# A one-core two-layer hybrid kernel: gathered-row dots pinned to program order and paced anew, gather credits raised, modulation rows placed elsewhere

## The chip, the cores and the metric

The kernel runs on one core of one Trainium2 chip, so all engines named below (TensorE = PE, VectorE = DVE, ScalarE = ACT, GpSimd = POOL, SyncE = SP) are those of a single core. The metric is the device time of one execution in microseconds (us); the median of repeated runs is compared.

## The reference

Two layers, each a mixer followed by a feed-forward part, on 512 tokens of width 1024. Layer 0 mixes with a gated linear recurrence (LRU), layer 1 with an attention with a forget gate (FoX). Both feed-forward parts are PEER: each token picks 16 of 16,384 experts for each of 8 heads, and an expert is one row of `u` and one row of `v`. Ahead of each part the token is normed and modulated by a shift, a scale and a gate that come from one vector `c`.

```python
for layer in range(DEPTH):
    shift, scale, gate = ada_modulation(c, mw, mb)     # silu(c) @ mw + mb
    h = rms_norm(x, g) * (1.0 + scale) + shift
    x = x + gate * mixer(h, ...)                       # rglru or fox
    shift, scale, gate = ada_modulation(c, mw2, mb2)
    h = rms_norm(x, g2) * (1.0 + scale) + shift
    x = x + gate * peer_ffn(h, ...)

# peer_ffn, for 128 tokens:
q = (xc @ q_w).reshape(TOKEN_CHUNK, PEER_HEADS, 2, PEER_HALF)
...                                                    # two top-16 searches, then top-16 of sums
expert = e1 * PEER_KEYS + e2                           # 128 experts for each token
g = jax.nn.softmax(top_s, axis=-1)
u = jnp.take(expert_u, expert, axis=0)
act = gelu(jnp.einsum('thkd,td->thk', u, xc))
w = g * act
return jnp.einsum('thk,thkd->td', w, jnp.take(expert_v, expert, axis=0))
```

## The kernel before

The 512 tokens are four tiles of 128. PEER treats them in two ways. For the first three tiles (`nd` = 3) it computes **all** experts densely: 128 blocks of 128 experts each, where a block's up-projection (`pacc`, L509 to L511, three matmul terms of split fp32) gives activations, these are multiplied by a dense table of gates, and the result is multiplied by the block of `v` into `vacc` (L1263). For the last tile (t = 3) it **gathers** instead (`gathered`): POOL issues an indirect DMA for each of the 128 picked rows of `u` (L1141), DVE takes the dot of that row with the token (L1154), and later the same for 128 rows of `v`, which DVE accumulates with a weight (L1171). The gathered rows live in a ring of 8 buffers (`RING`).

A third way stands in between: the last 32 rows of tile 2 (`XT`) are not in the dense table but go through `looked_up`: 32 dots (L1031) of rows that POOL gathers (L1016), first into 13 borrowed buffers, then into a small pool `xr` of three.

PEER runs in stages. First come the queries. Then comes the **gates stage**: 68 of the blocks (`NFIRST`) have their up-projection computed early and stored to HBM (`ascr`), and beside them run the routes (top-k searches on DVE), the three `dense_gates` generators and `looked_up`. `dense_gates(t)` builds the table for one token tile from batches of 16 tokens: DVE makes one-hot tiles `p2` and `p1` by comparing with an iota (L1115, L1118), multiplies `p1` with the gates in two precisions into two `pg` tiles (L1126; `gp`, L1084 and L1085, is the gates' split), and PE multiplies them (L1100). Then comes the **expert loop** over 128 blocks in which a block's activations are loaded back (`at<-ascr`, on ACT's queue) or computed, multiplied with the gate tile `gtile` (L1249), split (L1253 on ACT, L1256 on DVE) and multiplied by `v` (L1263). Every weight of the dense products is split into `whi` (ACT, L185) and `wlo` (DVE, L187).

Three kinds of side work are written as generators and mixed into these loops by credit. A `Background` holds a list of generators; `pump(credit)` adds credit and runs units until it is spent, and each unit costs what it yields. `GP` is the credit per stored block in the gates stage; `PUMPS` holds for each layer the credit per block of the expert loop (first number: block not stored; second: block stored). `between_steps(main, side, (a, b))` runs `looked_up` as the side of the other generators: each side unit costs a before `xr` exists, and b after it. What is left at a loop's end is run by `bg.finish()` right there, ahead of the work that follows.

The third kind is the modulation: one dot of a 1024-long weight row `mw` with `c` for each of 128 outputs (L220, then one or two small column operations L224 to L227), and one load of 0.5 MB for each row on POOL's queue (`mod_gen`). `AT` cuts the 24 rows of `l1_mix` into those done in the LRU's output projection, those in the first PEER's loop (`between`), and the rest; `M1` does the same for the 6 first rows of `l1_ffn`, which are done after the first PEER's gathered rows (`last_rows`).

The kernel is scheduled by a framework that may move an instruction ahead of others on its engine; `keep_in_program_order` (often called `pin`) forbids that. At run time each engine's queue is in order: an instruction that waits for a DMA holds all behind it.

## Time and profile before

| | |
|---|---|
| median of 3 runs | 3128.37 us (3125.5 to 3131.63) |
| profiled execution | 3128.77 us |
| its span in the trace | 3127.0 us (so 1.8 us lie outside it) |
| ScalarE busy | 1490.6 us (48%) |
| GpSimd busy | 1055.3 us (34%) |
| DMA moved | 855.28 MB, mean 274 GB/s |

In the trace the stages of layer 0 lie at about 0 to 205 us (norm and LRU), 205 to 270 (LRU's output projection), 270 to 440 (norm and PEER's queries), 440 to 775 (gates stage), 775 to 1500 (expert loop). FoX follows to 1824, with its output projection to 1870; the second PEER has its queries up to 2040, its gates stage from 2040 to 2365 and its expert loop from 2365 to 3105. The last stretch to 3127 is the end of that loop's adds and the stores.

How to read it: PE is busy most of the time in every stage, so what counts is where PE stands still and who releases it. A row of the timeline gives start, duration, engine, line, operation and tile, and in brackets the idle time ahead of the instruction on its engine with the work that ended it. A row of the windows gives a stretch, its length, then for each engine the busy us and the number of instructions, then the granted clock of PE, the busy share of the DMA engines, and GB/s.

### The profile page before, as it was taken

How to read it: one execution, taken by the hardware profiler on the slowest of the kernel's cores; microseconds unless marked ns; L12 is line 12 of the kernel's file. 1: busy time of each engine (PE TensorE's matmuls, PEld its weight loads, DVE VectorE, ACT ScalarE, POOL GpSimd, SP SyncE). 2: the span in 40 equal slices, each digit the busy share in tenths (PEclk: the TensorE clock that was granted, in tenths of full speed). 3: DMA queues.
4: the chain of work that ended last, by engine and by line, in shares of the span. 5: the costliest groups of instructions: out<-in, count | busy, mean ns of one | idle time of the engine just before them, and what ended most of it. 6: DMA issues, size and time to landing. Idle time of an engine off the chain costs nothing.

```text
span 3127.0 us, 45280 instructions
## 1 busy us (share of the span) xinstructions
PE 2981.9 (95%) x16232; PEld 2624.3 (84%) x16232; DVE 2623.0 (84%) x5368; ACT 1490.6 (48%) x2432; POOL 1055.3 (34%) x906
## 2 busy tenths in 40 slices
PE   8999999988999999999999999999889999999996
PEld 6777899978888888888777778899888888888885
DVE  7867989877889889989779968898877888888888
ACT  6654244676333333333458843255684333433331
POOL 1001433201655525655011003422104444445454
PEclk9998999999999999999999999999999999999998
DMA  7554248877999999999532123377879999999998
GB/s 291 173 184 172 101 152 293 294 248 258 413 376 397 380 352 393 373 364 348 190 119 82 62 108 117 125 267 263 271 247 372 362 350 366 366 358 370 355 335 291
DMA packets 307938, 855.28 MB, mean 274 GB/s; under 512 B 27296, under 2 KB 162496, under 8 KB 268928
## 3 DMA queue, kind: packets, MB, share of 16 engines
q1 hardware_dynamic: 67280, 388.77, 32.9%
q0 software_dynamic: 98624, 354.99, 30.3%
q10 hardware_dynamic: 141808, 108.63, 10.5%
q8 instruction: 127, 2.08, 0.3%
q14 instruction: 99, 0.81, 0.1%
HBM read 767.93 MB, written 83.51 MB: 272 GB/s over the span
## 4 chain that ended last, share of the span: by engine, by line
PE 42%; DVE 25%; issue 15%; DMA 10%; ACT 4%; POOL 3%; ACTq 0%; DVEq 0%; SPq 0%; POOLq 0%
PE vacc L1263 16%; DMA at<-ascr 6%; PE pacc L511 6%; PE pacc L509 6%; PE pacc L510 6%; DVE wlo L187 4%; DVE accg L1171 3%; DVE rows L1154 2%; POOL rows L1141 2%; DVE pg L1126 2%; DMA rowx<-in_l_u_dram,eix 1%; DVE p L1118 1%; POOL rowx L1016 1%; DVE p L1115 1%; DVE mw L220 1%
## 5 line engine op out<-in xcount | busy, mean ns | idle before, releaser
L511 PE MATMUL pacc<-hhi,wlo 128*128 128x352 f32 (+1 forms) x2600 | 891.7, 343 | 15.4 <-DVE wlo L187 14.7
L509 PE MATMUL pacc<-hhi,whi 128*128 128x352 f32 (+1 forms) x2600 | 895.6, 344 | 9.7 <-ACT at L1242 6.9
L185 ACT ACTIVATE whi<-wraw 128x1024 fp32r<-128x1024 f32 (+1 forms) x646 | 662.0, 1032 | 481.3 <-PE pacc L510 271.1
L510 PE MATMUL pacc<-hlo,whi 128*128 128x352 f32 (+1 forms) x2600 | 889.1, 342 | 0.0
L187 DVE TENSOR_TENSOR wlo<-wraw,whi 128x1024 fp32r<-128x1024 f32 (+2 forms) x580 | 698.7, 1211 | 143.0 <-ACT whi L185 140.7
L1263 PE MATMUL vacc<-wlo,wh 128*128 128x512 f32 x1536 | 599.2, 390 | 4.9 <-DVE wlo L187 4.9
L1263 PE MATMUL vacc<-whi,wh 128*128 128x512 f32 x1536 | 599.4, 390 | 1.6 <-ACT wh L1253 0.9
L1263 PE MATMUL vacc<-whi,wl 128*128 128x512 f32 x1536 | 598.7, 390 | 0.0
L511 PEld LDWEIGHTS pacc<-hhi,wlo 128*128 128x128 f32 x2600 | 493.4, 190 | 45.4 <-DVE wlo L187 22.4
L509 PEld LDWEIGHTS pacc<-hhi,whi 128*128 128x128 f32 x2600 | 494.3, 190 | 36.6 <-ACT at L1242 7.8
L510 PEld LDWEIGHTS pacc<-hlo,whi 128*128 128x128 f32 x2600 | 495.4, 191 | 25.9
L1253 ACT ACTIVATE wh<-at 128x384 fp32r<-128x384 f32 x256 | 134.2, 526 | 778.2 <-DVE at L1249 611.7
L1141 POOL DMA_INDIRECT rows<-in_l_v_dram,ei x256 | 375.4, 1466 | 324.8 <-DVE accg L1171 273.5
L1141 POOL DMA_INDIRECT rows<-in_l_u_dram,ei x256 | 367.9, 1437 | 301.8 <-DVE rows L1154 251.8
L1263 PEld LDWEIGHTS vacc<-wlo,wh 128*128 128x128 f32 x1536 | 289.4, 188 | 62.6 <-DVE wlo L187 6.8
L1263 PEld LDWEIGHTS vacc<-whi,wl 128*128 128x128 f32 x1536 | 288.9, 188 | 60.3
L1263 PEld LDWEIGHTS vacc<-whi,wh 128*128 128x128 f32 x1536 | 288.9, 188 | 58.5 <-ACT wh L1253 1.3
L1171 DVE SCALAR_TENSOR_TENSOR accg<-rows,act,accg 128x1024 f32<-128x1024 f32 x254 | 324.8, 1279 | 0.6
L1154 DVE SCALAR_TENSOR_TENSOR rows<-rows,hn 128x1024 f32<-128x1024 f32 x256 | 305.2, 1219 | 2.4 <-issue 1.2
L1249 DVE TENSOR_TENSOR at<-at,gtile 128x384 f32<-128x384 f32 x256 | 141.1, 553 | 168.5 <-DMA at<-ascr 155.3
L1102 ACT ACTIVATE st<-gps 128x512 f32<-128x512 f32 x192 | 185.4, 1111 | 40.0 <-PE gps L1100 28.2
L187 POOL TENSOR_TENSOR wlo<-wraw,whi 128x1024 fp32r<-128x1024 f32 (+1 forms) x62 | 125.3, 2032 | 181.4 <-ACT whi L185 181.4
(335 smaller groups left out, 3639.4 us busy)
## 6 DMA issues: line engine op xcount, KB each, us to landing
wraw<-in_l_uT_dram SPq DMA_DIRECT2D x128, 1024.0 KB
wraw<-in_l_vp_dram SPq DMA_DIRECT2D x128, 1024.0 KB
gscr<-st ACTq DMA_DIRECT2D x48, 1024.0 KB
gtile<-gscr SPq DMA_DIRECT2D x90, 512.0 KB
mw<-in_l_ffn_mw_dram POOLq DMA_DIRECT2D x48, 512.0 KB
ascr<-at ACTq DMA_DIRECT2D x136, 176.0 KB
at<-ascr ACTq DMA_DIRECT2D x136, 176.0 KB
mw<-in_l_mix_mw_dram POOLq DMA_DIRECT2D x32, 512.0 KB
```

Of the source, the lines that this page charges most:

```text
L185: self.pin(nc.scalar.activation(hi, raw, AF.Copy))
L187: self.pin((nc.gpsimd if self.on_pool else nc.vector).tensor_sub(lo, raw, hi))
L509: nc.tensor.matmul(ps, whi[:, k, :], hhi[:, k, :n], start=(k == 0), stop=False)
L510: nc.tensor.matmul(ps, whi[:, k, :], hlo[:, k, :n], start=False, stop=False)
L511: nc.tensor.matmul(ps, wlo[:, k, :], hhi[:, k, :n], start=False, stop=(k == KD - 1))
L1102: A.activation(st[:, :, q * 4:q * 4 + 4].rearrange("p e t -> p t e"), gps, AF.Copy, scale=1.0 / GSCALE)
L1141: i = nc.gpsimd.indirect_dma_start(out=rows, out_offset=None, in_=src, in_offset=bass.IndirectOffsetOnAxis(ap=ei[:, j:j + 1], axis=0))
L1154: V.scalar_tensor_tensor(r, r, 1.0, hn, op0=OP.mult, op1=OP.mult, accum_out=act[:, j:j + 1]))
L1171: i = V.scalar_tensor_tensor(acc, r, w, acc, op0=OP.mult, op1=OP.add)
L1249: pin(V.tensor_tensor(at.rearrange("p (b t) -> p b t", t=16), at.rearrange("p (b t) -> p b t", t=16), gts[c // 8][:, :, c % 8, :], op=OP.m ...
L1253: pin(A.activation(wh, at, AF.Copy))
L1263: T.matmul(acc[t][d], x[:, ts], y[:, d, :], start=(i == 0 and x is wh and y is vh), stop=(i == PK - 1 and x is wl))
```

## The change

Counts of instructions on each engine stay the same. The change does four things. It raises the credits of the expert loops (`PUMPS`) and of the gates stage (`GP`), with slightly higher costs for the route's units. It changes the side credits of `looked_up` from (6.2, 4.2) to (6.8, 3.3), adds two empty units to it, and pins its dots and the operations of `dense_gates` to program order. It moves two modulation rows of `l1_mix` from the LRU's output projection into the first PEER's loop, gives those that stay four buffers and a delay by credit (`later`). And it moves the first six rows of `l1_ffn` from the end of the first PEER to the output projection of FoX.

```diff
--- before.py
+++ after.py
@@ -37,15 +37,15 @@
 XT = 32
 EARLY = (4, 0, 0, 2, 0, 2, 2, 2)
 NEARLY = sum(EARLY)
-PUMPS = ((4.45, 1.4), (3.9, 1.2))
+PUMPS = ((4.55, 1.5), (4.2, 1.35))
 AHEAD = 6
-GP = 5.2
+GP = 5.35
 GSCALE = 32768.0
 M1 = 6
 RING = 8
 MB = 2
 LP = 1.55
-AT = (4, 14)
+AT = (4, 12)
 
 
 class Ctx:
@@ -228,6 +228,10 @@
         if k + bufs < len(rows):
             got.append(load(rows[k + bufs]))
         yield unit
+
+
+def later(credit):
+    yield credit
 
 
 def row_of(g, psum, col, name):
@@ -959,14 +963,14 @@
             V.tensor_tensor(ge2, ge, row[:, :n], op=OP.mult)
             V.tensor_tensor(ge, ge, tab[0], op=OP.mult)
             fold(ge, n, ranks(e[0], q))
-            yield (5.5, 6.6)[q]
+            yield (6.0, 7.2)[q]
             j = rs.tile([128, HK], BF, name="j", tag="j")
             fold(ge2, n, j.rearrange("p (h k) -> p h k", h=PH))
             V.tensor_sub(j, posb, j)
             V.tensor_tensor(ge, j.unsqueeze(1).to_broadcast(shp), col[:, :n], op=OP.is_equal)
             V.tensor_tensor(ge, ge, tab[1], op=OP.mult)
             fold(ge, n, ranks(e[1], q))
-            yield (5.0, 7.6)[q]
+            yield (5.5, 8.4)[q]
 
         def route(t):
 
@@ -985,11 +989,12 @@
                 ei = (pk if t >= nd else rt).tile([128, 128], I32, name="ei", tag="ei" if t >= nd else "back")
                 V.scalar_tensor_tensor(ei, e[0], float(PK), e[1], op0=OP.mult, op1=OP.add)
                 e.append(ei)
-            yield 2.0
+            yield 2.2
 
         def looked_up(t, pu, pw, psum):
 
 
+            pin = tc.keep_in_program_order
             gt, ei = routes[t][2:]
             own = slice(128 - XT, 128)
 
@@ -1023,17 +1028,19 @@
             for s in range(SG - 1):
                 nc.scalar.dma_start(hn[s * XT:(s + 1) * XT], hn[own])
             yield 0.1
+            yield 0.1
             for j in range(XT):
                 for _ in range(2):
                     if len(rows) < (XT if "xr" in env else 13):
                         fetch(len(rows))
                 r = rows[j]
-                V.scalar_tensor_tensor(r, r, 1.0, hn, op0=OP.mult, op1=OP.mult, accum_out=act[:, j:j + 1])
-                yield 1.35 if "xr" in env else 2.7
+                pin(V.scalar_tensor_tensor(r, r, 1.0, hn, op0=OP.mult, op1=OP.mult, accum_out=act[:, j:j + 1]))
+                yield 1.35 if "xr" in env else 2.9
             A.activation(act, act, AF.Gelu)
             back = rt.tile([128, 128], F32, name="back", tag="back")
             for s in range(SG):
                 nc.scalar.dma_start(back[own, s * XT:(s + 1) * XT], act[s * XT:(s + 1) * XT])
+            yield 0.1
             V.tensor_mul(back[own], back[own], gt[own])
             most = rt.tile([128, 1], F32, name="mostc")
             V.memset(most, 1.0)
@@ -1081,8 +1088,9 @@
             for w in range(2):
                 A.activation(edup[w], tp[:, w, :].unsqueeze(2).to_broadcast(shp), AF.Copy)
             gp = [pu.tile([128, 128], F16, name=f"gp{i}", tag=f"gp{i}") for i in range(2)]
-            V.tensor_scalar(gp[0], tp[:, 2, :], GSCALE, None, op0=OP.mult)
-            V.scalar_tensor_tensor(gp[1], tp[:, 2, :], GSCALE, gp[0], op0=OP.mult, op1=OP.subtract)
+            pin = tc.keep_in_program_order
+            pin(V.tensor_scalar(gp[0], tp[:, 2, :], GSCALE, None, op0=OP.mult))
+            pin(V.scalar_tensor_tensor(gp[1], tp[:, 2, :], GSCALE, gp[0], op0=OP.mult, op1=OP.subtract))
             gdup = []
             for i in range(2):
                 d = pu.tile(shp, F16, name=f"gdup{i}", tag=f"gdup{i}")
@@ -1112,10 +1120,10 @@
                 def spread(x):
                     return x[:, bs, :].unsqueeze(1).to_broadcast(shp)
                 p2 = pw.tile(shp, F16, name="p2", tag="p2")
-                V.tensor_tensor(p2, iota_e.unsqueeze(1).to_broadcast(shp),
-                                edup[1][:, bs, :].unsqueeze(2).to_broadcast(shp), op=OP.is_equal)
+                pin(V.tensor_tensor(p2, iota_e.unsqueeze(1).to_broadcast(shp),
+                                    edup[1][:, bs, :].unsqueeze(2).to_broadcast(shp), op=OP.is_equal))
                 p1 = pu.tile(shp, F16, name="p1", tag="p1")
-                V.tensor_tensor(p1, it, spread(edup[0]), op=OP.is_equal)
+                pin(V.tensor_tensor(p1, it, spread(edup[0]), op=OP.is_equal))
                 yield 2.4
                 if todo:
                     products(*todo.pop())
@@ -1123,7 +1131,7 @@
                 pg = []
                 for i in range(2):
                     x = pw.tile(shp, F16, name=f"pg{i}", tag=f"pg{i}")
-                    V.tensor_tensor(x, p1, spread(gdup[i]), op=OP.mult)
+                    pin(V.tensor_tensor(x, p1, spread(gdup[i]), op=OP.mult))
                     pg.append(x)
                     yield 1.15
                 todo.append((t * 8 + b, p2, pg))
@@ -1201,7 +1209,7 @@
                 todo = []
                 order = (nd - 1, *range(nd - 1), *range(nd, TC))
                 parts = [*[route(t) for t in order], *[dense_gates(t, pu, pw, psum, todo) for t in range(nd)]]
-                bg = Background(parts[0], between_steps(itertools.chain(*parts[1:-1]), looked_up(nd - 1, pu, pw, psum), (6.2, 4.2)),
+                bg = Background(parts[0], between_steps(itertools.chain(*parts[1:-1]), looked_up(nd - 1, pu, pw, psum), (6.8, 3.3)),
                                 parts[-1])
                 for c in FIRST[NEARLY:]:
                     first_up(banks, c)
@@ -1626,12 +1634,12 @@
         vectors(*subs[1:])
         lru(g, h, head, *arg("lru_", "conv", "bias", "lam"),
             lambda p: (mod("l0_mix", p, gate, MB), mod("l0_ffn", p, first, MB), mod("l1_mix", p, every[:AT[0]], MB)),
-            grow("l0_mix"), lambda p: (mod("l1_mix", p, every[AT[0]:AT[1]]),))
+            grow("l0_mix"), lambda p: (later(2.4), mod("l1_mix", p, every[AT[0]:AT[1]], 4)))
         peer(g, normed("l0_ffn"), flat("l0_u"), flat("l0_v"), grow("l0_ffn"),
              lambda p: mod("l0_ffn", p, gate, 4, ring=8), lambda p: mod("l1_mix", p, every[AT[1]:], 4, ring=8),
-             lambda p: mod("l1_ffn", p, first[:M1], 4, ring=8), 3, PUMPS[0])
+             None, 3, PUMPS[0])
         fox(g, normed("l1_mix"), *arg("fox_", "fb", "qg", "kg"), lambda p: (mod("l1_ffn", p, first[M1:], 1),),
-            grow("l1_mix"), lambda p: ())
+            grow("l1_mix"), lambda p: (later(2.4), mod("l1_ffn", p, first[:M1], 4)))
         peer(g, normed("l1_ffn"), flat("l1_u"), flat("l1_v"), grow("l1_ffn"),
              lambda p: mod("l1_ffn", p, gate, 4, ring=8), None, None, 3, PUMPS[1])
         drop_x(g)
```

The instructions move on DVE at many places. The first shown is the gates stage of the first PEER, where `dense_gates` of token tile 0 ends and that of tile 1 begins (`rowx` is a gathered row, `p` a one-hot tile, `pg` its product with the gates). Before:

```order
L187 TENSOR_TENSOR wlo<-wraw,whi 128x1024
L1031 SCALAR_TENSOR_TENSOR rowx,actx<-rowx,hn 128x1024 x4
L187 TENSOR_TENSOR wlo<-wraw,whi 128x1024
L1031 SCALAR_TENSOR_TENSOR rowx,actx<-rowx,hn 128x1024 x3
L1118 TENSOR_TENSOR p_6469<-iota_f,edup_6455 128x2048
L1084 TENSOR_SCALAR gp_6459<-tp 128x128
L1115 TENSOR_TENSOR p_6467<-iota_f,edup_6456 128x2048
L1085 SCALAR_TENSOR_TENSOR gp_6460<-tp,gp_6459 128x128
L187 TENSOR_TENSOR wlo<-wraw,whi 128x1024
L1126 TENSOR_TENSOR pg_6547<-p_6469,gdup_6463 128x2048
```

After (line numbers are shifted: L1037 was L1031, L1134 was L1126, L1123 and L1126 were L1115 and L1118, L1092 and L1093 were L1084 and L1085):

```order
L1037 SCALAR_TENSOR_TENSOR rowx,actx<-rowx,hn 128x1024
L187 TENSOR_TENSOR wlo<-wraw,whi 128x1024
L1134 TENSOR_TENSOR pg_6387<-p_6305,gdup_5694 128x2048
L1123 TENSOR_TENSOR p_6389<-iota_f,edup_5685 128x2048
L1126 TENSOR_TENSOR p_6391<-iota_f,edup_5684 128x2048
L1037 SCALAR_TENSOR_TENSOR rowx,actx<-rowx,hn 128x1024
L1134 TENSOR_TENSOR pg_6437<-p_6391,gdup_5692 128x2048
L187 TENSOR_TENSOR wlo<-wraw,whi 128x1024
L1134 TENSOR_TENSOR pg_6471<-p_6391,gdup_5694 128x2048
L1092 TENSOR_SCALAR gp_6481<-tp 128x128
L1093 SCALAR_TENSOR_TENSOR gp_6482<-tp,gp_6481 128x128
L1037 SCALAR_TENSOR_TENSOR rowx,actx<-rowx,hn 128x1024
```

Seven dots stood in two runs ahead of the next tile's first one-hot operations; now there is one dot between two one-hot or product operations, and the gates' split `gp` follows the last `pg` of the tile before.

The second place is the end of the second PEER's expert loop on DVE (`accg` is the sum of the gathered `v` rows, `gt` and `x` are the final gated adds). Before:

```order
L1171 SCALAR_TENSOR_TENSOR accg<-rows,act,accg 128x1024
L1256 TENSOR_TENSOR wl<-at_30322,wh 128x384
L1171 SCALAR_TENSOR_TENSOR accg<-rows,act,accg 128x1024
L187 TENSOR_TENSOR wlo<-wraw,whi 128x1024
L1171 SCALAR_TENSOR_TENSOR accg<-rows,act,accg 128x1024 x13
L521 TENSOR_TENSOR gt<-accg,grow 128x512
L522 TENSOR_TENSOR x_30492<-x_30492,gt 128x512
```

After (L1179 was L1171, L525 and L526 were L521 and L522, L1257 and L1264 were L1249 and L1256):

```order
L1179 SCALAR_TENSOR_TENSOR accg<-rows,act,accg 128x1024
L1264 TENSOR_TENSOR wl<-at_30311,wh 128x384
L1257 TENSOR_TENSOR at_30359<-at_30359,gtile 128x384
L187 TENSOR_TENSOR wlo<-wraw,whi 128x1024
L1257 TENSOR_TENSOR at_30388<-at_30388,gtile 128x384
L1264 TENSOR_TENSOR wl<-at_30359,wh 128x384
L187 TENSOR_TENSOR wlo<-wraw,whi 128x1024
L1264 TENSOR_TENSOR wl<-at_30388,wh 128x384
L187 TENSOR_TENSOR wlo<-wraw,whi 128x1024 x2
L525 TENSOR_TENSOR gt<-accg,grow 128x512
L526 TENSOR_TENSOR x_30492<-x_30492,gt 128x512
```

The 13 accumulations that stood behind the last `wlo` have moved ahead of the last blocks' own operations, and the adds follow the last `wlo` at once.

The third place is the start of the adds in FoX's output projection on DVE (`oacc` is the projection's result). Before:

```order
L521 TENSOR_TENSOR gt<-oacc_17982,grow 128x512
L187 TENSOR_TENSOR wlo<-wraw,whi 128x1024
L522 TENSOR_TENSOR x_17971<-x_17971,gt 128x512
L521 TENSOR_TENSOR gt<-oacc_17983,grow 128x512
L522 TENSOR_TENSOR x_17973<-x_17973,gt 128x512
L521 TENSOR_TENSOR gt<-oacc_17984,grow 128x512
L522 TENSOR_TENSOR x_17975<-x_17975,gt 128x512
L521 TENSOR_TENSOR gt<-oacc_17985,grow 128x512
```

After:

```order
L525 TENSOR_TENSOR gt<-oacc_17949,grow 128x512
L187 TENSOR_TENSOR wlo<-wraw,whi 128x1024
L526 TENSOR_TENSOR x_17938<-x_17938,gt 128x512
L220 SCALAR_TENSOR_TENSOR mw,mdot<-mw,sc 128x1024
L227 TENSOR_TENSOR col_l_ffn_153<-mdot,bias_l_ffn 128x1
L525 TENSOR_TENSOR gt<-oacc_17950,grow 128x512
L526 TENSOR_TENSOR x_17940<-x_17940,gt 128x512
L220 SCALAR_TENSOR_TENSOR mw,mdot<-mw,sc 128x1024
L187 TENSOR_TENSOR wlo<-wraw,whi 128x1024
L224 TENSOR_SCALAR mdot<-mdot,bias_l_ffn 128x1
L225 TENSOR_TENSOR col_l_ffn_161<-mdot,gain_l_ffn 128x1
```

Modulation dots (L220) with their small operations now stand between the adds, six in all up to the norm of the second PEER. The same six stood between `wlo`, `wl` and `at` at the end of the first PEER's loop, and stand there no more. On POOL the six loads `mw<-l_ffn` moved from ahead of the first PEER's four `x<-xs` loads to behind FoX's four.

## Prediction

> **What bounds the kernel now.** I read the page first: the span and the slices of PE, DVE and DMA; then a table of windows, one row for each stage that the change touches; then the waits of PE and DVE, longest first.
>
> ```profile
> span 3127.0 us, 45280 instructions
> PE 2981.9 (95%) x16232; PEld 2624.3 (84%) x16232; DVE 2623.0 (84%) x5368; ACT 1490.6 (48%) x2432; POOL 1055.3 (34%) x906
> ...
> PE   8999999988999999999999999999889999999996
> DVE  7867989877889889989779968898877888888888
> DMA  7554248877999999999532123377879999999998
> ```
> ```profile
> 440.00:775.00 335.00, 303.65 (x2307) 293.95 (x2307) 277.87 (x494) 214.87 (x291) 52.20 (x46) 0.96 0.79 265
> 775.00:1500.00 725.00, 717.17 (x3511) 627.80 (x3510) 641.34 (x862) 272.31 (x480) 386.10 (x283) 0.99 0.97 375
> 2040.00:2365.00 325.00, 295.42 (x2251) 286.18 (x2250) 268.97 (x437) 211.12 (x284) 49.23 (x37) 0.95 0.79 266
> 2365.00:3105.00 740.00, 735.67 (x3614) 642.54 (x3613) 630.90 (x836) 276.14 (x485) 371.27 (x267) 1.00 0.94 357
> ```
> ```profile
> PE gps L1100 <- DVE pg L1126: 37.3, 18, 8.2
> ...
> PE vacc L1263 <- DVE wlo L187: 4.9, 4, 2.5
> ```
> ```profile
> DVE at L1249 <- DMA at<-ascr: 155.3, 48, 5.5
> ...
> DVE rowx L1031 <- DMA rowx<-in_l_u_dram,eix: 35.7, 16, 7.1
> ```
>
> PE bounds it, and no work of PE is removed. PE stands still for 3127.0 − 2981.9 = 145 us, and only these can be won. By stage they are 335 − 303.65 = 31 us in the first gates stage, 7.8 in the first expert loop, 30 in the second gates stage, 4.3 in the second loop, some 22 behind PE's end, and about 50 in norms and mixers. So the gates stages and the end are worth the most; the expert loops, which the new credits are about, can hardly be won and can be lost: DVE is 85 to 88% busy there (641.34 of 725, 630.90 of 740) and the DMA engines 97 and 94%. The longest wait of PE is for `pg` (37.3 us, 18 times), and DVE, which makes `pg`, itself waits 35.7 us for gathered rows of `looked_up`.
>
> **The change part by part.** Gains are negative. The sum is made against the profiled execution, 3128.77 us, which is 0.4 above the median.
>
> *A. LRU's output projection, two modulation rows fewer.*
>
> ```profile
> 267.36 1.23 DVE L220 SCALAR_TENSOR_TENSOR mw<-mw,sc 128x1024 f32<-128x1024 f32 x1 [2.57 <-DMA mw<-in_l_mix_mw_dram]
> ...
> 268.51 0.69 DVE L521 TENSOR_TENSOR gt<-oacc,grow 128x512 f32<-128x512 f32 x1
> ```
> ```profile
> 272.70 1.09 PE L448 MATMUL xa<-ident,xn 128*128 128x128 f32 x8 [2.89 <-DVE xn L421]
> 275.03 1.97 PE L448 MATMUL xa<-ident,xn 128*128 128x128 f32 x8 [1.24 <-DVE xn L421]
> 277.99 1.97 PE L448 MATMUL xa<-ident,xn 128*128 128x128 f32 x8 [0.99 <-DVE xn L421]
> ```
>
> The add of the second half (L521) stands behind a dot that waited 2.57 us for its row and took 1.23. PE then lacks `xn` for 2.89 + 1.24 + 0.99 = 5.1 us. With eight rows in four buffers, loaded sooner, the 2.57 + 1.23 = 3.8 us go: **−4**. Bounds: −7 (the 5.1 and PE's half clock behind them) and 0 (the norm's own chain is late in any case).
>
> *B and F. The two gates stages.* Of the first one:
>
> ```profile
> 560.15 1.23 DVE L1031 SCALAR_TENSOR_TENSOR rowx<-rowx,hn 128x1024 f32<-128x1024 f32 x1 [3.12 <-DMA rowx<-in_l_u_dram,eix]
> ...
> 623.02 1.23 DVE L1031 SCALAR_TENSOR_TENSOR rowx<-rowx,hn 128x1024 f32<-128x1024 f32 x1 [6.25 <-DMA rowx<-in_l_u_dram,eix]
> ...
> 629.75 1.23 DVE L1031 SCALAR_TENSOR_TENSOR rowx<-rowx,hn 128x1024 f32<-128x1024 f32 x1 [2.06 <-DMA rowx<-in_l_u_dram,eix]
> ...
> 686.33 1.23 DVE L187 TENSOR_TENSOR wlo<-wraw,whi 128x1024 fp32r<-128x1024 f32 x1 [5.35 <-ACT whi L185]
> ```
> ```profile
> 564.11 0.38 PE L1100 MATMUL gps<-pg,p 128*128 128x128 f16 x4 [4.25 <-DVE pg L1126]
> 635.98 0.29 PE L1100 MATMUL gps<-pg,p 128*128 128x128 f16 x1 [8.17 <-DVE pg L1126]
> ```
>
> A run of dots ahead of a tile's first one-hots empties the ring of gathered rows; DVE stands (3.12; 6.25 and 2.06), and behind it `p`, `gp`, `pg`. PE then waits 4.25 and 8.17 us. The same places in the second layer:
>
> ```profile
> 2156.79 0.58 PE L1100 MATMUL gps<-pg,p 128*128 128x128 f16 x4 [5.79 <-DVE pg L1126]
> 2229.17 0.29 PE L1100 MATMUL gps<-pg,p 128*128 128x128 f16 x1 [8.06 <-DVE pg L1126]
> ```
>
> A gap costs more than itself, since the granted clock (third column from the end) is near half behind it:
>
> ```profile
> 636.00:640.00 4.00, 4.00 (x27) 3.32 (x28) 4.00 (x4) 4.00 (x7) 0.00 (x0) 0.54 0.78 292
> 2229.00:2233.00 4.00, 3.83 (x22) 3.15 (x23) 4.00 (x5) 4.00 (x7) 0.00 (x0) 0.50 0.81 292
> ```
>
> That is 4 × 0.46 = 1.8 us and 4 × 0.50 = 2.0; I take the same behind the shorter gap of each layer. So the gaps are worth 4.25 + 8.17 + 3.7 = 16.1 in the first layer and 5.79 + 8.06 + 4.0 = 17.9 in the second. By the change's order one dot stands between two one-hot operations, so a gather has several DVE instructions of 1.2 us to land in, and `gp` follows the last `pg`. I take 85%: **−14** and **−15**, 15% staying since some dot will still meet a late row. DVE has the room (335 − 277.87 = 57 us idle in the stage, and waits like the 5.35 us ahead of L187 at 686 fall where the next tile could have begun). Bounds for each: −5 (PE waits as long in smaller pieces) and −22 (also what now is lost to `pg` at the stage's end goes).
>
> *D. First PEER's end: six modulation dots gone.*
>
> ```profile
> 1507.53 1.22 DVE L220 SCALAR_TENSOR_TENSOR mw<-mw,sc 128x1024 f32<-128x1024 f32 x1
> ```
> ```profile
> 1511.70 0.50 PE L1263 MATMUL vacc<-wlo,wh 128*128 128x512 f32 x1 [2.50 <-DVE wlo L187]
> ```
> ```profile
> 1513.00:1520.00 7.00, 5.87 (x14) 4.16 (x14) 5.72 (x10) 2.19 (x5) 0.57 (x1) 0.53 0.47 151
> ```
>
> Four such dots stand among the last blocks' `wlo`, `wl` and `at`; PE waits up to 2.50 us for `wlo`, and the clock then is 0.53 for 7 us, worth 7 × 0.47 = 3.3. The two together are 5.8; I take **−5**. Bounds: −6 and −2 (the clock drop stays).
>
> [...]
>
> *E. FoX's output projection: six dots more.*
>
> ```profile
> 1840.00:1860.00 20.00, 20.00 (x87) 16.14 (x86) 9.96 (x13) 6.15 (x12) 0.00 (x0) 1.00 0.15 54
> ```
>
> Six dots of 1.23 are 7.4 us and their small operations 2. Their cover is DVE's idle 10.04 us in this one window, and the six loads (3 MB) find the DMA engines 85% idle. One dot stands behind the last add, ahead of the next chain: **+2** for it. Bounds 0 and +6 (half of the 9.4 is not covered).
>
> *G. Expert loops, denser gathers.*
>
> ```profile
> L1171 DVE SCALAR_TENSOR_TENSOR accg<-rows,act,accg 128x1024 f32<-128x1024 f32 x254 | 324.8, 1279 | 0.6
> ```
>
> In layer 1 the 13 accumulations behind the last `wlo` move into the loop: 13 × 1.279 = 16.6 us of DVE, and 13 × 0.5 MB = 6.8 MB, 19 us at 357 GB/s. There are 740 − 631 = 109 us of idle DVE and 6% of 740 = 44 us of idle DMA. So on average they fit, but DVE's queue is in order and its idle time is mostly the wait for `at`, so part of them pushes a `wlo`. I take a quarter: +4. In layer 0 the total stays, except two modulation rows more (1 MB, 2.8 us at 375 GB/s), but the dots stand denser: +3. Together **+7**; bounds 0 and +22 (16.6 + 2.8 + 3).
>
> [...]
>
> *H. The end.*
>
> ```profile
> 3094.88 17.12 DVE L1171 SCALAR_TENSOR_TENSOR accg<-rows,act,accg 128x1024 f32<-128x1024 f32 x13
> ...
> 3114.17 0.69 DVE L522 TENSOR_TENSOR x<-x,gt 128x512 f32<-128x512 f32 x1 [1.45 <-DMA x<-xs]
> ...
> 3122.62 1.28 DVE L522 TENSOR_TENSOR x<-x,gt 128x512 f32<-128x512 f32 x2
> ```
> ```profile
> 3105.12 0.39 PE L1263 MATMUL vacc<-whi,wl 128*128 128x512 f32 x1
> ```
>
> PE ends at 3105.5, but DVE is at its 13 accumulations until 3112.0, and the adds end at 3123.9; the stores take 3.1 more. With the accumulations out of the way, the adds of three tiles run while PE does its last blocks, and behind PE's end stand one product (0.69), two adds (1.28) and the store (3.1): 3105.5 + 0.1 + 5.1 = 3110.7 instead of 3127.0: **−16**. Late next is PE itself. Bounds −11 (the last `wlo` and `at` that now stand behind the accumulations are late for PE) and −18.
>
> The sum: −4 − 14 − 15 − 5 + 2 + 7 − 16 = −45, and 3128.8 − 45 = **3084**.
>
> **The rivals.**
>
> *R1: the gates stages keep their loss.* `looked_up` still has 32 gathers in few buffers, and if each spaced dot waits a little, PE waits in many pieces. For it speaks that DVE waited 16 times for rows, not only at the two runs; against it that the long gaps all stand at runs. B and F then give −5 each: −45 + 19 = −26; with G at +12 besides, 3108.
>
> *R2: all goes.* G at 0, A −7, B and F −20 each, E 0, D −6, H −17: −70, 3059. For it: DVE's idle time in the gates stages; against it: DVE's share in the loops.
>
> *R3, slower: the loops' DVE waits reach PE.* DVE waits 155.3 us for `at<-ascr` in 48 waits, and today PE feels four `wlo` waits, 4.9 us, 1.2 each. Denser gathers delay the `at` loads on the same DMA engines, already 97% busy, and fill DVE's slack with dots, so that after each wait a `wlo` is late. If all 48 cost PE 1.2 us, G is 48 × 1.2 = 58 and the rest −52: 3135. At 2.5, the longest, it is 120: 3197. From G = 58 on the kernel is slower by over 0.2%. Against it: the loops' PE loss today is 12.1 us in all. I take 3145.
>
> *R4: the credits change little on the chip.* Where queues and not credits set the pace, the gather ends as late as now and the spread dots wait as before: 3122 to 3132. The order speaks against it at the end, where the accumulations have moved.
>
> **How the numbers follow.** Forecast 0.60; R1 0.18; R2 0.10; R3 0.07; R4 0.05. About 0.2% (6 us) is what a measurement of this kernel can tell from no change. Faster: 0.60 + 0.18 + 0.10 = 0.88; same 0.05; slower 0.07. The forecast's own range, with G, B and F at their bounds one at a time, is 3068 to 3100; to hold 8 in 10 the range takes in R1 and R2's edge: 3060 to 3116.
>
> **What would show it.** B and F: no wait of PE for `pg` above 3 us at the change of token tiles, DVE's wait for `rowx` well below 35.7 us, and no clock near 0.5 there. D: no `wlo` wait above 1 us at the first loop's end. H: no accumulation behind the last `wlo`, and under 7 us between PE's end and the span's. G: PE's idle time in the two loops, 12.1 us now, should be near 19; if it is above 60, the forecast is wrong by R3. If PE's idle time in the gates stages stays above 25 us each, it is wrong by R1.

## The result and the profile after

| | before | changed |
|---|---|---|
| median | 3129.05 us (5 runs, 3125.5 to 3131.83) | 3114.07 us (5 runs, 3111.14 to 3115.05) |
| profiled execution | 3128.77 us | 3111.14 us |
| its span | 3127.0 us | 3109.4 us |

The ratio is 0.9949 with the interval 0.9934 to 0.9963, so the change makes the kernel faster by about 16 us (12 to 21), where 45 were forecast. From L228 on, line numbers of the changed kernel are 4 to 8 higher.

Its page (busy time, share and count of each engine) and its windows for the same four stages as before, cut at the stages' own ends:

```profile
PE 2987.0 (96%) x16232; PEld 2631.3 (85%) x16232; DVE 2618.9 (84%) x5368; ACT 1486.9 (48%) x2432; POOL 1053.1 (34%) x906
```
```profile
424.00:766.00 342.00, 314.94 (x2323) 305.36 (x2323) 282.13 (x510) 215.35 (x293) 56.51 (x47) 0.94 0.77 258
766.00:1513.00 747.00, 734.28 (x3603) 640.80 (x3602) 660.40 (x896) 280.20 (x497) 387.88 (x282) 1.00 0.94 369
2018.00:2361.00 343.00, 312.14 (x2324) 301.55 (x2323) 282.48 (x508) 215.68 (x293) 55.11 (x47) 0.95 0.78 260
2361.00:3104.00 743.00, 735.48 (x3601) 641.98 (x3599) 642.75 (x850) 273.87 (x483) 366.07 (x266) 1.00 0.94 361
```

The span shrank by 17.6 us, and yet PE is busy 5 us longer for the same matmuls. The work of PE marks the stages well: I take the start of the last matmul of the norm's transposes, of the last score matmul of the queries, of the first and the last matmul of the expert loop, and so on. The differences between those marks, worked out from the two traces, are the account of the change:

| stage, us | before | changed | difference | forecast |
|---|---|---|---|---|
| LRU, its projection, first norm | 288.9 | 275.0 | −13.9 | A −4 |
| first queries | 148.4 | 148.9 | +0.6 | 0 |
| first gates stage | 338.0 | 342.4 | +4.4 | B −14 |
| first expert loop | 754.1 | 746.9 | −7.2 | D −5, G +3 |
| FoX and its projection | 340.7 | 340.7 | +0.1 | 0 |
| norm of the second PEER | 11.4 | 14.6 | +3.2 | E +2 |
| second queries | 148.4 | 149.0 | +0.6 | 0 |
| second gates stage | 337.1 | 343.2 | +6.1 | F −15 |
| second expert loop | 738.1 | 743.2 | +5.0 | G +4 |
| behind the last matmul | 21.9 | 5.4 | −16.4 | H −16 |

Five rows came out in the direction forecast; the two gates stages went the other way, 39.5 us off the forecast, more than all that is missing (the norm and the first loop gave more than was counted). These are single traces, and the gates stages scatter (see the start of the experiments): that the two stages did not shrink by 14 and 15 us is clear, that they grew is less so. What do they wait for now? First the waits of DVE and PE in the changed kernel (us in total, times, longest):

```profile
DVE at L1257 <- DMA at<-ascr: 144.9, 48, 6.1
...
DVE gp L1092 <- ACT edup L1089: 17.1, 3, 8.0
```
```profile
PE gps L1108 <- DVE pg L1134: 32.8, 22, 4.1
...
PE gps L1108 <- ACT st L1110: 8.5, 14, 1.7
```

The wait of DVE for gathered rows (35.7 us, 16 times before) is gone from the list altogether, as the spacing of the dots promised. In its place DVE waits for `edup`, a tile that ACT makes. And PE's wait for `pg` has only gone from 37.3 us in 18 times to 32.8 in 22: the gaps are shorter (4.1 at most, not 8.2) and more. Two windows of the changed kernel show what that does to PE's clock (third column from the end):

```profile
624.00:634.00 10.00, 8.38 (x55) 7.70 (x56) 10.00 (x10) 6.25 (x10) 2.38 (x2) 0.66 0.82 242
652.00:660.00 8.00, 5.80 (x45) 5.05 (x45) 6.49 (x8) 6.24 (x9) 1.39 (x1) 0.79 1.12 350
```

The first stands behind gaps of 2.63 and 1.42 us, the second among gaps of 0.87, 0.68 and 0.65. Split by matmul (start to next start, against the median for its kind), the first gates stage before is 290 us of matmuls, 31.3 of gaps and 16.5 of matmuls that ran slow; now it is 292, 27.1 and 23.0. So four microseconds of gaps were won, and more than that lost to the clock.

The place where the new wait begins is on ACT. The timeline of the changed kernel in the first gates stage (ACTq is ACT's own instruction queue; start, duration, and the idle time with its releaser):

```profile
582.78 8.00 ACTq L836 DMA_DIRECT2D ascr<-at  x1
590.82 1.06 ACT L185 ACTIVATE whi<-wraw 128x1024 fp32r<-128x1024 f32 x1 [8.03 <-issue]
...
613.61 5.37 ACTq L836 DMA_DIRECT2D ascr<-at  x1
619.02 1.94 ACT L1089 ACTIVATE edup<-tp 128x1024 f16<-128x1024 f32 x2 [5.67 <-issue]
```
```profile
591.91 1.23 DVE L187 TENSOR_TENSOR wlo<-wraw,whi 128x1024 fp32r<-128x1024 f32 x1 [3.98 <-ACT whi L185]
...
621.00 0.29 DVE L1092 TENSOR_SCALAR gp<-tp 128x128 f16<-128x128 f32 x1 [7.91 <-ACT edup L1089]
```
```profile
595.48 0.71 PE L1108 MATMUL gps<-pg,p 128*128 128x128 f16 x4 [4.14 <-DVE pg L1134]
624.20 0.43 PE L513 MATMUL pacc<-hhi,whi 128*128 128x352 f32 x1 [2.63 <-ACT at L835]
```

Read it from the left: ACT issues the store of an early block's activations (`ascr<-at`) right behind the 1 MB store of the gate table (`gscr<-st`), and stands at this issue for 8.00 us; its next split `whi` is that late; DVE's `wlo` waits for `whi`, the products `pg` are queued behind `wlo`, and PE waits 4.14 us for `pg`. At 613 it happens again, this time with `edup` of the next token tile. The group of these issues (ns, shortest, median and longest) shows that 8 us is not how long such an issue takes by itself:

```profile
L836 ACTq DMA_DIRECT2D ascr<-at x136: 321/327/7995, 278.4 to 2330.5; - x136
```

And the DMA queues of the changed kernel between 582.8 and 588 us (packets, MB, share of the 16 engines) show what went on meanwhile: ACT's queue (q10), with 1 MB of gate table waiting, moved 0.05 MB, while weights (q1) and gathered rows (q0) had the engines.

```profile
q1 hardware_dynamic: 102, 0.81, 70.1%
q0 software_dynamic: 81, 0.27, 13.7%
q10 hardware_dynamic: 106, 0.05, 3.4%
```

Of the 26 issues of this store that took over 0.9 us in the changed kernel, 25 came directly behind a store of the gate table on ACT's queue, and none later than 10 us after one. That the slow queue holds the issue is read from this; no run tests it by itself.

### The profile page after: what moved, and what is told of

It is laid out like the page before. It is cut to its first block, busy times and chain, and to the rows that moved or that the text cites. A ratio compares the mean times of both kernels' runs of the same rounds, so it can differ in the third digit from the quotient of the medians.

```text
span 3109.4 us, 45245 instructions
## 1 busy us (share of the span) xinstructions
PE 2987.0 (96%) x16232; PEld 2631.3 (85%) x16232; DVE 2618.9 (84%) x5368; ACT 1486.9 (48%) x2432; POOL 1053.1 (34%) x906
## 4 chain that ended last, share of the span: by engine, by line
PE 50%; DVE 23%; DMA 9%; issue 8%; ACT 8%; ACTq 2%; POOL 0%; DVEq 0%; SPq 0%; POOLq 0%
PE vacc L1271 16%; PE pacc L515 9%; PE pacc L513 9%; PE pacc L514 8%; DMA at<-ascr 7%; DVE wlo L187 4%; DVE accg L1179 4%; DVE rows L1162 3%; ACT st L1110 2%; DVE mw L220 1%; ACTq L836 1%; ACT whi L185 1%; PE gps L1108 1%; DVE at L1257 1%; DVE wl L1264 1%
## 5 line engine op out<-in xcount | busy, mean ns | idle before, releaser
L1179 DVE SCALAR_TENSOR_TENSOR accg<-rows,act,accg 128x1024 f32<-128x1024 f32 x254 | 324.4, 1277 | 0.1
L1257 DVE TENSOR_TENSOR at<-at,gtile 128x384 f32<-128x384 f32 x256 | 140.8, 552 | 151.8 <-DMA at<-ascr 144.9
L1021 POOL DMA_INDIRECT rowx<-in_l_u_dram,eix x52 | 75.5, 1452 | 354.7 <-DVE rowx L1037 187.5
```

The lines of the kernel that those rows point to most:

```text
L1179: i = V.scalar_tensor_tensor(acc, r, w, acc, op0=OP.mult, op1=OP.add)
L1257: pin(V.tensor_tensor(at.rearrange("p (b t) -> p b t", t=16), at.rearrange("p (b t) -> p b t", t=16), gts[c // 8][:, :, c % 8, :], op=OP.m ...
```

## The experiments

Two theories stood at the start. **Q**: ACT, standing at the issue of its stores, makes the gates stages long. **P**: the new pins do, because DVE must wait where it had other work to do. Each experiment is an edit of the changed kernel (e5 of the kernel before); stage times below are from its trace. For the scatter: the same FoX stage took 340.6 to 341.0 us in all but one of the traces (342.3), but the gates stages scatter more. The changed kernel, e6, e7 and e8 have the same gates code, and their second gates stages take 339.7 to 346.3 us; e12 and e17 turned out to have the same instructions, and theirs take 326.9 and 336.2. So one trace tells a difference of some 10 us in a stage and no less, and the median time is the safer number. The kernel before, timed again beside each group of runs, had medians of 3124 to 3132 us, so a few us between groups say nothing.

**All edits of the gates stages taken back (e1).**

```diff
-GP = 5.35
+GP = 5.2
-                bg = Background(parts[0], between_steps(..., (6.8, 3.3)),
+                bg = Background(parts[0], between_steps(..., (6.2, 4.2)),
...
```
(with the routes' credits, the empty units and all pins of these stages)

> The changed kernel with every edit of the gates stages taken back (gates and route credits, side credits, pins, the two empty units); pumps of the expert loops and the modulation rows stay as changed. If the gates edits cost what the stage marks say (4.4 us in the first layer, 6.2 in the second), this is about 10 us faster than the changed kernel: 3103 to 3106, and the stages take about 338 and 337 us again. If the longer stages come from elsewhere (another phase of the queues after the earlier start), the stages stay at 342 and 343 and the time at 3112 to 3116.

Measured: 3102.22 us (3099.41 to 3105.91), ratio to before 0.9924 (0.9906 to 0.9943), stages of 341.5 and 338.7. By the medians the whole of the gates edits costs about 12 us, by the ratios to before 8, with intervals that overlap by a little; the stages of the two traces differ by less than their scatter. So the rest of the change alone was probably the better kernel.

**The early stores issued by SP (e2).**

```diff
-            nc.scalar.dma_start(ascr[FIRST.index(c)], at)
+            nc.sync.dma_start(ascr[FIRST.index(c)], at)
```

> The changed kernel with the stores of the early activations (ascr<-at) issued by SP instead of ACT. Theory Q (ACT stands at the issue of this store while its queue still works off the gate table's store, and so is late with the next tile's one-hot inputs): ACT's issues of 2 to 8 us go, VectorE's wait for edup falls from 17.1 us to under 8, the two gates stages get 5 to 12 us shorter each: 3092 to 3104. Rival P (the pinned order makes VectorE wait at gp while it has dots to do): no change, 3111 to 3116. Rival: the stores hold up SP's weight loads: slower than 3116.

Measured: 3078.17 us (3072.94 to 3082.57), ratio to before 0.985 (0.9829 to 0.987). This is 36 us faster than the changed kernel by the medians (31 by the ratios to before), more than Q expected. The gates stages take 327.1 and 325.3 us. Its windows of the first stage, its wait of PE for `pg`, its wait of DVE for `edup`, and the issues of the stores, now on SP:

```profile
424.00:752.00 328.00, 308.11 (x2333) 298.82 (x2332) 281.72 (x513) 217.53 (x296) 57.21 (x48) 0.96 0.81 271
```
```profile
PE gps L1108 <- DVE pg L1134: 20.3, 19, 2.7
```
```profile
DVE gp L1092 <- ACT edup L1089: 5.3, 2, 2.7
```
```profile
L836 SPq DMA_DIRECT2D ascr<-at x136: 319/320/1401, 278.6 to 2299.0; - x136
```

DVE's work in the stage is the same 282 us, in 328 us and not 342; the DMA engines are busier (0.81, not 0.77), so it was never their total that was short. The longest wait for `pg` is now 2.7 us, that for `edup` fell from 8.0 to 2.7, and no issue of the store takes more than 1.4 us.

**No pins in the gates stages (e4).**

```diff
-            pin = tc.keep_in_program_order
+            pin = lambda x: x
```
(in `looked_up` and in `dense_gates`)

> The changed kernel without the pins of the dots and of the one-hot operations and products; credits and units stay. Rival P: VectorE does dots while edup is late, the stages get 4 to 8 us shorter each: 3098 to 3106. Theory Q: within 4 us of the changed kernel, 3110 to 3118, and ACT's issues of 2 to 8 us stay.

Measured: 3089.73 us (3086.21 to 3091.68); stages of 327.8 and 328.4 us. P expected 3098 to 3106, so its direction is right, and the gain is larger than it claimed. ACT's long issues are fewer but not gone (over 0.9 us: 22 us in the first stage, 40 in the changed kernel). And a run of dots is back, at the change from tile 0 to tile 1, with a long gap behind it, longer than the 8.17 us of before. PE there, and DVE's wait for rows:

```profile
628.02 0.27 PE L1108 MATMUL gps<-pg,p 128*128 128x128 f16 x1 [11.31 <-ACT st L1110]
```
```profile
DVE rowx L1037 <- DMA rowx<-in_l_u_dram,eix: 32.2, 22, 3.1
```

A gap of 11 us, and yet a short stage. PE's gaps in the first stage add up to 25.9 us, hardly less than the changed kernel's 27.1; what went is about 12 us of slow matmuls.

In the gates stages e4 differs from e1 only in credits and the two empty units: the new credits without pins made the kernel 12 us faster (3102 to 3090 by the medians, ranges that do not overlap), and the pins then cost 24 (3090 to 3114).

**The same stores on SP in the kernel before (e5).** The edit of e2 on the old kernel.

> The kernel before with the same stores issued by SP. Theory Q for the old order too (ACT stood 31 us at these issues in the first gates stage): 5 to 10 us faster than before, 3119 to 3124. If in the old order VectorE's waits for gathered rows set the pace and ACT's issues lay beside them: within 4 us of 3129.

Measured: 3131.15 us (3120.61 to 3135.55), ratio 1.0006 (0.9992 to 1.0021): nothing. There DVE waits for rows as before:

```profile
DVE rowx L1031 <- DMA rowx<-in_l_u_dram,eix: 41.0, 20, 6.1
```

So ACT's stores alone are not what holds the old kernel. It would be natural to say that DVE's waits for rows then hold it, but e10, next, keeps such waits and is short.

**Neither pins nor stores on ACT (e10).** The edits of e2 and e4 together.

> The changed kernel without the pins and with the stores on SP. Theory Q, with pins needed: without them a run of dots stands at the change of token tiles again (11 us there in the run without pins), so this is no better than the pinned kernel with the stores on SP, 3076 to 3086. If pins and stores cost separately, the two gains add (24 and 36): 3054 to 3066.

Measured: 3078.94 us (3075.84 to 3085.9); stages of 329.0 and 328.0. The gains of e2 and e4 do not add. So the loss of the changed kernel needs both: a late ACT, and an order that lets PE feel it. DVE's wait for rows and PE's for `pg` in this run:

```profile
DVE rowx L1037 <- DMA rowx<-in_l_u_dram,eix: 29.6, 16, 5.4
```
```profile
PE gps L1108 <- DVE pg L1134: 36.9, 19, 10.4
```

Both are nearly as they were before the change, and the kernel is as fast as e2, which has neither the wait for rows nor a long gap. So with the new credits these waits cost nothing that can be told. In the gates stages e10 differs from e5 only in credits and the two empty units, and its two stages together are 17 us shorter; how the credits do it no run shows.

**Which pins? (e11, e12)** In e11 the pins of the 32 dots alone are away, in e12 those of `dense_gates` alone.

```diff
-            pin = tc.keep_in_program_order
+            pin = lambda x: x
```
(e11 in `looked_up`, e12 in `dense_gates`)

> The changed kernel without the pins of the 32 dots alone; the one-hot operations and products stay pinned. If the dots' pins are what costs (the stages were 14 us shorter each with no pins at all), 3086 to 3096, with a run of dots at the change of token tiles. If the pins of the one-hot operations cost, near the changed kernel: 3108 to 3116.

> The changed kernel without the pins of the gates' split, the one-hot operations and the products; the dots stay pinned. If these pins cost (VectorE is held at gp until edup is there), 3086 to 3096. If the dots' pins cost, 3108 to 3116.

Measured: e11 3104.95 us (3091.0 to 3109.14), stages of 339.4 and 336.0; e12 3087.05 us (3086.23 to 3090.24), stages of 330.6 and 326.9. It is the pins of `dense_gates`: without them 27 us are won, although ACT's long issues are nearly as many (33 us over 0.9 in the first stage). In e12 PE waits for `pg`:

```profile
PE gps L1108 <- DVE pg L1134: 17.9, 13, 4.6
```

In e12 the dots alone are pinned, and DVE's wait for rows falls to 0.2 us in all, from 32.2 in e4, which has no pin. The medians are 3087 and 3090, in ranges that overlap: pinning the dots alone took the waits away and won 3 us or nothing.

e11 lies between the two expectations, with one run far below its others; it settles nothing by itself.

**Which of the pinned operations? (e15, e16, e17)** In all three the dots are pinned; of `dense_gates` only the one-hot tiles (e15), only the products (e16), only the gates' split (e17).

```diff
-            pin = tc.keep_in_program_order
+            pin = lambda x: x
...
-                pin(V.tensor_tensor(p1, it, spread(edup[0]), op=OP.is_equal))
+                tc.keep_in_program_order(V.tensor_tensor(p1, it, spread(edup[0]), op=OP.is_equal))
```
(e15, with the same for `p2`; e16 and e17 do it for the products and for the split)

> Dots pinned as changed; of the gates' operations only the two one-hot tiles are pinned, the gates' split and the products are free. If the one-hots' pins cost (the one that can be made early must wait its turn behind a dot or a product): 3106 to 3116. If not: 3084 to 3092, as with no gates pins (3087).

> Dots pinned; of the gates' operations only the two products are pinned. If their pins cost: 3106 to 3116. If not: 3084 to 3092.

> Dots pinned; of the gates' operations only the split of the gates (gp) is pinned, at which VectorE waited 7.9 and 8.0 us for edup in the changed kernel. If that pin costs: about 16 us and the clock behind, 3100 to 3112. If not: 3084 to 3092.

Measured: e15 3116.09 us (3107.85 to 3124.07), stages of 345.0 and 340.3; e16 3089.87 us (3088.34 to 3098.89), 330.0 and 335.1; e17 3090.76 us (3084.71 to 3094.55), 328.7 and 336.2. It is the pins of the one-hot tiles. The pin of the split changes nothing at all: e17's instructions are those of e12, one by one, so e17 is a repetition of e12. In e15, with the gates' split free, DVE waits for `edup` at `gp` as in the changed kernel; in e17, with it pinned, hardly. First e15, then e17:

```profile
DVE gp L1092 <- ACT edup L1089: 18.6, 4, 8.2
```
```profile
DVE gp L1092 <- ACT edup L1089: 0.8, 1, 0.8
```

So the 17.1 us in the changed kernel's list stand at `gp` but come with the one-hots' order. How a pin on DVE can make ACT late shows in the order of ACT's instructions at the change from tile 0 to tile 1. First the changed kernel (e15 has the same), then e12 (e16 and e17 have the same):

```
L835 ACTIVATE at<-pacc 128x352
L1111 ACTIVATE gtile<-st 128x128
L1112 DMA gscr_2356<-st 128x16x128
L836 DMA ascr<-at 128x352
L1089 ACTIVATE edup_6477<-tp 128x1024
```
```
L1110 ACTIVATE st<-gps 128x4x128 x4
L836 DMA ascr<-at 128x352
L1111 ACTIVATE gtile<-st 128x128
L1112 DMA gscr_2356<-st 128x16x128
L1089 ACTIVATE edup_6477<-tp 128x1024
```

With the one-hots pinned the scheduler puts the small store right behind the large one and `edup` behind both, so that `edup` pays the long issue (5.37 us at 613.61, `edup` at 619.02); with them free the small store goes ahead of the large one (in e12 0.33 us at 611.54, the large one 0.38 at 614.28), and `edup` follows at 614.71. This joins Q and P: the pins changed the order on an engine that they do not name. Over the whole program e16 and e17 give ACT the order of e12, and e15 that of the changed kernel but for one small operation in each layer. Between these two orders more differs in the gates stages, a few instructions on ACT and many on DVE, and no run tells what each of them costs. The wait at `gp` is not all of it: in e11, and in e3 below, the one-hots are pinned and this wait is down to 2.3 and 3.1 us, yet they take 3105 and 3110 us.

**Old credits with the new pins (e3).**

```diff
-GP = 5.35
+GP = 5.2
-                bg = Background(parts[0], between_steps(..., (6.8, 3.3)),
+                bg = Background(parts[0], between_steps(..., (6.2, 4.2)),
```

> The changed kernel with the old side credits of looked_up (6.2, 4.2) and the old gates credit (5.2), pins kept. If spacing and pace by credit are what removes VectorE's waits for gathered rows, these waits come back (from 0 towards 35 us) on top of the pins' cost: 3118 to 3130. If the pins alone space the dots: no waits for rows and 3108 to 3117.

The routes' costs and the empty units stay as changed. Measured: 3109.71 us (3104.72 to 3116.09); DVE's list has no wait for gathered rows. So the pins space the dots, not these credits. With all pins in place these credits win nothing that can be told; the 12 us between e1 and e4 are won without pins.

**Old credits of the expert loops (e6).**

```diff
-PUMPS = ((4.55, 1.5), (4.2, 1.35))
+PUMPS = ((4.45, 1.4), (3.9, 1.2))
```

> The changed kernel with the old credits of the expert loops. If the end's gain is all theirs, the last dots stand behind PE's end again (the stretch from the last matmul to the span's end back from 5.4 to some 21 us) and the second loop gives back some 5 us: 3121 to 3128. If the end's gain has another source (order, POOL's queue), the stretch stays near 5 us and the time within 5 us of the changed kernel's 3114.

Measured: 3123.88 us (3120.78 to 3134.12); behind the last matmul 19.9 us, not 5.4. The end's gain is theirs, and the second loop (741.4) did not get shorter in a way that can be told.

**Old place of the two `l1_mix` rows (e7).**

```diff
-AT = (4, 12)
+AT = (4, 14)
-            grow("l0_mix"), lambda p: (later(2.4), mod("l1_mix", p, every[AT[0]:AT[1]], 4)))
+            grow("l0_mix"), lambda p: (mod("l1_mix", p, every[AT[0]:AT[1]]),))
```

> The changed kernel with the two modulation rows back in the LRU's output projection, two buffers and no delay. By the stage marks this place gained 14 us (up to the end of the norm's transposes, 289 to 275 us): 3124 to 3130. By the prediction's term A it was worth 4: 3116 to 3120.

Measured: 3123.22 us (3106.38 to 3127.23); up to the first norm's end 286.4 us, where the changed kernel has 275.0. Over all traces this stretch takes 286.4 to 288.9 us with the rows in the projection (3 traces) and 275.0 to 279.5 without (14). So about 11 of the 14 us of this place are the rows', three times the term. A dot waits again for its row ahead of the last adds, in e7:

```profile
265.82 1.22 DVE L220 SCALAR_TENSOR_TENSOR mw<-mw,sc 128x1024 f32<-128x1024 f32 x1 [2.23 <-DMA mw<-in_l_mix_mw_dram]
```

**Old place of the six `l1_ffn` rows (e8).**

```diff
-             None, 3, PUMPS[0])
+             lambda p: mod("l1_ffn", p, first[:M1], 4, ring=8), 3, PUMPS[0])
...
-            grow("l1_mix"), lambda p: (later(2.4), mod("l1_ffn", p, first[:M1], 4)))
+            grow("l1_mix"), lambda p: ())
```

> The changed kernel with the six modulation rows back at the first PEER's end. Terms D and E: the first loop's end loses 5 to 8 us again, the norm of the second PEER wins back 3: 3115 to 3121. If the first loop's gain came from its credits instead: 3108 to 3113.

Measured: 3108.73 us (3102.17 to 3117.32), 5 us faster than the changed kernel's median and within the scatter of it. The norm of the second PEER is back at 11.4 us (14.6 with the rows there). The first loop took 751.0 us; over all traces it takes 755.1 in the mean with the six rows at its end (before, e5, e8, e14: 751.0 to 758.9) and 749.9 without (13 traces, 746.9 to 757.1). By these means the move wins about 5 us in one place and loses 3 in the other, but the ranges overlap, and the time of e8 lies where it was expected if the first loop's gain came from its credits and not from the rows. What the move is worth in the first loop stays open.

**A version with the pieces that hold (e14).** The stores on SP, the small copies `back<-actx` on SP too, and the six rows at their old place.

```diff
-                nc.scalar.dma_start(back[own, s * XT:(s + 1) * XT], act[s * XT:(s + 1) * XT])
+                nc.sync.dma_start(back[own, s * XT:(s + 1) * XT], act[s * XT:(s + 1) * XT])
```

> The changed kernel with the early stores and the small copies of the looked-up activations (back<-actx, for which VectorE waited 11.2 us in two waits with the stores alone on SP) issued by SP, and the six modulation rows back at the first PEER's end, as those cost 3 us in the second norm and won nothing that could be told in the first loop. Against the kernel with the stores on SP (3078): 3 us less from the norm, 3 to 8 us less from the copies: 3066 to 3074. If the six rows do cost the first loop's end: 3074 to 3080.

Measured: 3073.84 us (six runs, 3070.94 to 3090.78), ratio to before 0.9824 (0.9801 to 0.9848). It is the fastest median of all and in its expected interval, but the intervals of e2 and e14 overlap; that the copies or the rows matter beside the stores is not shown.

## Why the prediction was wrong, step by step

**B and F failed**: "I take 85%: −14 and −15". The wait named for the loss (runs of dots, DVE waiting for gathered rows) was real, and the pins removed it: 35.7 us of waits to none. The step that failed is the next one, that with this wait gone PE would have its `pg`, and that each stage would get shorter by 85% of PE's gaps there and of the slow matmuls behind them. The runs showed three things in its place.

- The waits for rows were worth far less than the gaps behind them. Pins that take them away (e4 to e12, 32.2 us of waits to 0.2) won 3 us or nothing, and with the stores on SP (e10 to e2, 29.6 us to none) 1 us or nothing, where 29 were forecast. A pin moves other instructions too (ACT's long issues in the first stage add up to 22 us in e4 and 33 in e12), so a cost of the pins may hide part of the gain; and both pairs have the new credits, as no run pins the dots alone with the old ones.
- The pins of the one-hot tiles, with ACT's stores of the early blocks as they are, cost some 25 us by the medians (e12, e16 and e17 against e15 and the changed kernel), and moving these stores off ACT gives that back and more (e2). "DVE has the room" was argued from DVE's idle time alone; what ACT would be doing at that moment was never asked, though ACT feeds DVE with `whi` and `edup` in every batch.
- The credits of these stages (with the two empty units), which have no price of their own in B and F, won 12 us where nothing was pinned (e1 to e4). Why is open.

With the stores on SP the stages are 327.1 and 325.3 us, 11 and 12 below before and near the forecast's 14 and 15. That is luck and no support for the forecast's mechanism, since e4 and e10 get to 328 and 329 us with DVE still waiting for rows. In the changed kernel itself they are at +4.4 and +6.1.

The trace of before showed the piece that was missed: ACT stood at an issue of this same store for 4.50 us at 615 us, beside the 6.25 us for which DVE waited for a row, and I took only the releaser that came last. An idle time put down to one releaser can hide another that ends just ahead of it.

```profile
615.02 4.50 ACTq L832 DMA_DIRECT2D ascr<-at  x1
```

The same stretch shows what DVE's order costs: by the order of the splits, the `wlo` that ran at 624.17 us had had its `whi` since 614.46, and stood behind the dot that got its row at 623.02.

The forecast's own range had a slip too: its 3068 needs B and F at their bounds together, and one at a time they reach 3076.

**R1** was the rival that came true in its result (the gates stages keep their loss, PE waits in many pieces; 27 and 31 us of gaps, above the 25 that was set as its sign) but not in its cause: it had the spaced dots wait for rows, and none does. Its time, 3108, was nearer than the forecast's.

**The clock** was counted in B and F for the long gaps only. The windows at 624 and 652 us show 0.66 and 0.79 with no gap above 2.63 us and none above 0.87. Over the whole first gates stage slow matmuls cost 23.0 us beside 27.1 us of gaps, of which the longest was 4.14, and before the change 16.5 us beside 31.3, of which the longest was 8.17: in these two traces the pieces of idle time cost no less clock than the long gaps. So R1's picture, a long gap cut into pieces, is worth less than nothing.

**A** was right in mechanism and too small: −4 against −13.9, of which e7 gives 11.4 to the rows. The term had only the wait of one dot. The windows of the same stretch, from the projection's last matmul to the norm's end, show the rest. First before, then changed:

```profile
269.00:289.00 20.00, 14.58 (x73) 12.96 (x72) 16.94 (x37) 14.06 (x25) 2.52 (x5) 0.74 0.25 95
```
```profile
263.00:275.00 12.00, 10.75 (x71) 9.61 (x70) 10.18 (x23) 10.83 (x20) 1.41 (x3) 1.00 0.30 105
```

The same matmuls take 12 us and not 20, at a clock of 1.00 and not 0.74. The bound of −7 was drawn with half a clock for the gaps alone; the clock stayed low for the whole norm. Some 4 us more were won in the projection itself.

**D and G in the first loop** gave −7.2 where −2 was the sum, in the right direction. D alone would be about −5 by the means over all traces, but these overlap, and e8's time speaks for the credits; how the gain is shared is open. At D's place no gap above 0.3 us is left ahead of the last matmul, and the clock is full:

```profile
1497.00:1504.00 7.00, 7.00 (x33) 5.79 (x32) 4.62 (x7) 2.51 (x5) 0.54 (x1) 1.00 0.43 147
```

**G in the second loop** was +5.0 in this trace against +4; over all traces the loop takes 740.8 us with the new credits (14 traces, 737.1 to 746.0) and 739.6 with the old (3 traces, 738.1 to 741.4), so its true size is nearer 1. R3 is out.

**E** was right: +3.2 against +2, and e8 takes it back. The dot behind the last add holds the next chain, as the prediction named it:

```profile
1858.24 1.22 DVE L220 SCALAR_TENSOR_TENSOR mw<-mw,sc 128x1024 f32<-128x1024 f32 x1
```
```profile
1860.23 0.67 PE L500 MATMUL pacc<-hhi,whi 128*128 128x352 f32 x2 [2.48 <-DVE hhi L447]
```

**H** was right to the microsecond in the trace: −16.4 against −16, with 5.1 us between PE's end and the span's, and e6 shows that it is the loops' credits. The last rows of DVE and PE in the changed kernel:

```profile
3089.22 1.23 DVE L187 TENSOR_TENSOR wlo<-wraw,whi 128x1024 fp32r<-128x1024 f32 x1 [2.38 <-ACT whi L185]
...
3104.99 1.28 DVE L526 TENSOR_TENSOR x<-x,gt 128x512 f32<-128x512 f32 x2
```
```profile
3103.96 0.39 PE L1271 MATMUL vacc<-whi,wl 128*128 128x512 f32 x1
```

## What to carry to other kernels

Price a wait by a run that takes it away, not by its length: here 32 us of DVE's waits for rows went, and the time changed by 3 us. When a wait goes, ask of every engine that feeds the waiting one what it was doing in that time, not only whether the waiting one has room. Pin an order only where it is needed, and look at the order of the other engines afterwards: the pins of the one-hot tiles on VectorE changed what ScalarE did first, and cost some 25 us, more than the new credits had won. Look at what stands ahead of a small store on the queue of an engine that computes for the path: here the issue of 176 KB took ACT up to 8.00 us right behind a store of 1 MB, and 0.33 us in the median of all.

## What the runs showed that was not expected

An issue of a 176 KB store took ACT 0.33 us in the median and 8.00 at the longest, with the same engine's 1 MB store ahead of it. With the 136 small stores moved to SP's queue, with the same bytes, the longest issue took 1.40 us, and the changed kernel was 31 to 36 us faster (e2); the same move made the kernel before no faster at all (e5, ratio 1.0006).

Cutting idle time of PE into smaller pieces did not keep its clock: in the first gates stage 4 us less of gaps came with 6.5 us more of slow matmuls.
